# A hybrid decoder step: the tokens of the second part in two halves, the recurrence over all heads for each half

## The chip, the cores and the metric

One core of one Trainium2 chip runs the whole step as one program. The metric is the device time of that program in microseconds; lower is better. The engines are named as in the profile: PE (TensorE products), PEld (its loads of weights), DVE (VectorE), ACT (ScalarE), POOL (GpSimd) and SP (SyncE, which here issues nearly every DMA).

## The reference

One layer, 1024 prompt tokens and 8 samples of 4 tokens each (1056 columns), width 1024, in float32:

```
z = rmsnorm(x) @ w_in                       # conv inputs, r k v and LoRA inputs, two gates
ya = silu(layernorm(dwconv31(glu))) @ w_conv_out
xs = z_r + (shifted(z_r) - z_r) * mu        # token shift, then r, k, v, decay w, a, g
S_t = S_{t-1} diag(w_t) + (S_{t-1} a_t) b_t^T + v_t k_t^T ;  y_t = S_t r_t   # per head, 16 heads of 64
yb = ((groupnorm(y) + bonus) * g) @ w_rw_out
x = x + (sig(g1) * ya + sig(g2) * yb) @ w_mix_out
up = rmsnorm(x) @ w_up ; cu = dwconv3(up) ; x = x + (gelu(cu_1) * cu_2) @ w_down
out = rmsnorm(x), and the new conv, shift, wkv and ffn states
```

Only the recurrence over `S_t` and the two causal convolutions tie a token to those before it. Everything after the recurrence works on tokens by themselves, but for the three taps of the feed-forward's convolution, which need two earlier columns.

## The kernel before

Products in float32 precision are three products of rounded halves: each operand is split into a high and a low part, and `mm3` (a helper; all its products stand on line 54) sums high x high, high x low and low x high. Weights come by tiles: `wjob` (L47 to L49) loads 512 KB into `wraw`, ACT writes the high part `whi`, POOL the low part `wlo`. A tile of the weights is multiplied with all 1056 tokens in three blocks of 352 columns.

The program has three stages. First the input norm and `mixer_a`: convolution inputs, its taps on DVE, the LoRA parts and r, k, v of the first two tiles of channels. Then `mixer_b`, the recurrence. It is cut into 16 steps `n`: two pairs of heads (`J = n // 4`) and a quarter of the prompt (`q = n % 4`, 256 tokens in four chunks of 64). A step goes through `prep` (decays P on L904, the operands E and BK), `stage` (products of the keys into LQ; then the inverses of the 32 x 32 diagonal blocks, by 31 pairs of DVE operations on `tm` and `X`, L1027 and L1029, with round trips through DRAM before and after), `combine`, `chain` (the recurrence over the four chunks, whose output `Yev` is written on L1152) and `group_norm`. E, BK and LQ lie in the pool `stage` with three buffers. The samples' recurrence and the layer norm of the convolution run beside it. Last comes the tail: the conv branch's output (`conv_out`), `merge`, `mix`, and the feed-forward `ffn` by groups of three tiles (`ffn_up`, `ffn_down`), with the final norm in `ffn_last`. Intermediate results of all tokens go through DRAM (`d_ma`, `d_x2`).

The order of `mixer_b` is set by a planner, `drive` (L701). It holds a list of streams, each a generator that yields the time for which it has to wait, and a clock that counts products alone. The first stream that is due gets its turn; where none is, a step of a filler product is put in between. Fillers are the 18 remaining tiles of r, k, v and the 16 tiles of the gates, which are held back by `due` until a chain far enough ahead is done. Step `n` is prepared only after `chain(n - 3)`. The planner only gives the order of emission; the framework's scheduler then places the instructions of each engine by that priority and by readiness, and the engines run them in order.

The waiting times of a step by the planner:

```
W_NIN, W_BV, W_GN, W_STAGE = 6000, 8000, 12000, 0     # ns, in prep and group_norm
TINV = 29750                                          # from the end of stage to combine
LAT = (950, 1050, 1200)                               # in chain, for each of four chunks, 800 ahead
if n > 2:
    k.append(("chain", n - 3))                        # s_prep
```

Of the kernel before, what the change touches and what calls it, by code (L numbers as in the profile page):

```python
# [18 lines left out]
NB = 3  # L19
# [11 lines left out]

class Net:
# [7 lines left out]
    # ---------------------------------------------------------------- helpers  # L40
# [34 lines left out]
    def project_g(self, w, x, nk, evac, m=128):  # L75
        """products of one tile of the weights with all tokens; yields after every step of the contraction"""
# [12 lines left out]
    def project(self, *a, **k):  # L89
        self.run(self.project_g(*a, **k))  # L90

    def split_tok(self, b, ps, prompt, sample):
        """block b of the tokens: prompt(columns, psum) and sample(psum as batch x 4)"""
        t0 = b * BW
        n = min(TP - t0, BW)
        prompt(t0, n, ps[:, :n])
        if n < BW:
            sample(ps[:, n:BW].rearrange("p (b t) -> p b t", t=4))

    # ------------------------------------------------------------------ build  # L100
    def build(self):
        with ExitStack() as es:
# [4 lines left out]
            self.hL = self.hp.tile([128, 8, T], F32R, name="hL")  # L107
            self.wp = self.pool(es, "weights", 2)
            with ExitStack() as e1:
                self.rp = self.pool(e1, "wraw", 1)  # L110
                with ExitStack() as e:
                    self.pm = self.pool(e1, "pm", 4, space=PSUM)
                    self.pw = self.pool(e1, "pw", 2, space=PSUM)
                    xs, w0 = self.load_in(e)
                    self.norm_in(e, xs)
                with ExitStack() as e:
                    self.t4 = self.pool(e, "t4", 8)
                    self.mixer_a(w0)
                self.mixer_b()
            self.rp = self.pool(es, "wraw2", 2)  # L120
            self.tail()

    def consts(self, e):
# [18 lines left out]
        # vectors: rows of 128 in DRAM, turned on the tensor engine  # L142
# [29 lines left out]
    def turn(self, gi):  # L172
        """vectors of a group, by partitions"""
# [23 lines left out]
    # --------------------------------------------------- input norm, transposed  # L197
# [53 lines left out]
    # ------------------------------------------------ first part of the mixer  # L251
    def mixer_a(self, w0):
# [9 lines left out]
        self.d_ma, self.d_ga, self.d_gb, self.d_y = dram("d_ma"), dram("d_ga"), dram("d_gb"), two("d_y")  # L262
# [29 lines left out]
    def weave(self, main, *aux):  # L292
        """steps of the products, and between them those of the others, each at its rate from when it is ready"""
# [18 lines left out]
    def conv_start(self, e):  # L312
        """histories of the samples, by rows"""
# [10 lines left out]
    def conv_proj(self, cv, i, w=None):  # L324
        """gated inputs of the convolution, tile i of the channels"""
# [24 lines left out]
    def conv_taps(self, cv, i):  # L350
# [11 lines left out]
        # samples: all taps, then their sum  # L362
# [7 lines left out]
        # new buffers  # L370
# [14 lines left out]
    NLN, LNW = 8, 132  # L385

    def ln_block(self, b):
        """layer norm of the convolution's channels and twice their silu, for one block of the tokens"""
        nc = self.nc
        W = self.LNW  # L390
        s = slice(b * W, (b + 1) * W)
# [3 lines left out]
        def fold(t):  # L395
            """sum of the four channel tiles, in Q"""
# [21 lines left out]
    def conv_in(self):  # L418
        """the conv branch's inputs, in the room of the recurrence"""
        nc = self.nc  # L420
        self.e_sg.close()
        self.cvp = self.pool(self.e_sg, "conv", side="right")
        self.cs = [self.cvp.tile([128, 4, T], F32R, name=f"cs{x}") for x in "HL"]
        for b in range(NB):
            s = slice(b * BW, (b + 1) * BW)
            c = self.cvp.tile([128, 4, BW], F32, tag="cs", name="cs", bufs=2)
            nc.sync.dma_start(out=c, in_=self.d_cs[:, :, s])
# [4 lines left out]
    def conv_out(self, i):  # L432
# [6 lines left out]
        if i < ND - 1:  # L439
            self.cw = job(i + 1)  # L440
# [1238 lines left out]
```

## Time and profile before

| | |
|---|---|
| median of 3 runs | 2597.11 us (2591.31 to 2606.79) |
| profiled execution, span | 2603.0 us; the page gives no other time for it |
| PE busy | 2437.3 us, 94% |
| DVE, ACT, POOL busy | 1535.1, 913.1 and 914.3 us |
| moved by DMA | 230.62 MB, 89 GB/s on average |

The profile is of one execution. Busy time is the time in which an engine has an instruction in flight. The granted clock is given as a share of the full 2.4 GHz; the half level is 1.2 GHz. Products are pipelined, so a busy PE isn't PE at its peak. Some records of products are missing (2568 of the large products with `hH` stand where the code issues more), so that durations are read from runs of them on the chain of waits. A row of a group of instructions has the line, the engine, the operation, output and inputs by the program's names, count, busy time and mean.

### The profile page before, as it was taken

What the parts mean: (1) busy time and instruction counts of PE and PEld (TensorE: products, weight loads), DVE (VectorE), ACT (ScalarE), POOL (GpSimd) and SP (SyncE); (2) the same over time, 40 slices, a digit from 0 to 9 for tenths busy, and PEclk for the clock granted to TensorE, in tenths of its full rate; (3) what the DMA queues carried; (4) which work ended last, traced back from release to release, by engine and by line L of the source; (5) the groups of instructions that cost most, each with busy time, mean ns of one, the idle gap of its engine ahead of it and who ended that gap; (6) DMA issues with size and microseconds to landing.
All of it is one profiled execution on the core that took longest, in us unless ns stands there. A gap on an engine that the chain in (4) does not pass through costs nothing.

```text
span 2603.0 us, 41626 instructions
## 1 busy us (share of the span) xinstructions
PE 2437.3 (94%) x16094; PEld 2182.3 (84%) x16094; DVE 1535.1 (59%) x3588; ACT 913.1 (35%) x1732; POOL 914.3 (35%) x879
## 2 busy tenths in 40 slices
PE   6899989989899889999898999999999999999998
PEld 5788977767787767777666899999999999999998
DVE  5999765677675866655655434455444435444445
ACT  4234342344254344344343412333222212222225
POOL 3432261334333524433232224333323323232343
PEclk9999977688786888787688999999999999999999
DMA  4124442233232333433333564441111111111111
GB/s 120 53 68 167 159 113 76 76 92 103 77 95 84 91 83 93 108 83 78 81 98 79 189 228 144 116 158 51 36 54 45 44 48 43 47 51 38 54 45 74
DMA packets 307638, 230.62 MB, mean 89 GB/s; under 512 B 90492, under 2 KB 287123, under 8 KB 306921
## 3 DMA queue, kind: packets, MB, share of 16 engines
q1 hardware_dynamic: 307185, 227.80, 29.8%
q8 instruction: 127, 2.08, 0.3%
q14 instruction: 70, 0.57, 0.1%
q0 software_dynamic: 256, 0.17, 0.0%
HBM read 157.45 MB, written 70.45 MB: 88 GB/s over the span
## 4 chain that ended last, share of the span: by engine, by line
PE 65%; DVE 14%; DMA 3%; issue 1%; SPq 1%; ACT 1%; POOL 1%; ACTq 0%; POOLq 0%; DVEq 0%
PE mm L54 51%; PE w L54 6%; DVE tm L1027 4%; DVE X L1029 4%; PE c L54 3%; PE y L54 3%; DMA L<-dL 2%; PE w L61 2%; DMA dX<-X 1%; DVE UV L1142 0%; DVE E L922 0%; DVE E L981 0%; SPq L1031 0%; DVE UV L1131 0%; DVE t L961 0%
## 5 line engine op out<-in xcount | busy, mean ns | idle before, releaser
L54 PE MATMUL mm<-hH,whi 128*128 128x352 f32 (+1 forms) x2568 | 900.6, 351 | 23.0 <-DVE bcol L496 13.1
L54 PE MATMUL mm<-hH,wlo 128*128 128x352 f32 (+1 forms) x2568 | 882.0, 343 | 0.0
L54 PE MATMUL mm<-hL,whi 128*128 128x352 f32 (+1 forms) x2568 | 880.6, 343 | 0.3 <-DVE hL L248 0.3
L54 PEld LDWEIGHTS mm<-hH,whi 128*128 128x128 f32 (+1 forms) x2568 | 508.3, 198 | 53.0 <-issue 20.1
L54 PEld LDWEIGHTS mm<-hL,whi 128*128 128x128 f32 (+1 forms) x2568 | 510.3, 199 | 13.4 <-issue 1.1
L54 PEld LDWEIGHTS mm<-hH,wlo 128*128 128x128 f32 (+1 forms) x2568 | 509.6, 198 | 13.3 <-issue 0.9
L49 POOL TENSOR_TENSOR wlo<-wraw,whi 128x1024 fp32r<-128x1024 f32 (+2 forms) x123 | 295.6, 2403 | 413.6 <-ACT whi L48 377.9
L48 ACT ACTIVATE whi<-wraw 128x1024 fp32r<-128x1024 f32 (+2 forms) x123 | 126.0, 1024 | 338.6 <-PE mm L54 231.7
L1541 DVE SCALAR_TENSOR_TENSOR c<-u,par,c 128x1024 f32<-128x1024 f32 x96 | 167.0, 1739 | 55.9 <-ACT c L1537 55.9
L1027 DVE TENSOR_TENSOR tm<-L,X 128x60 f32<-128x60 f32 (+24 forms) x496 | 168.0, 339 | 41.1 <-DMA L<-dL 33.5
L359 DVE SCALAR_TENSOR_TENSOR sg<-cu,par,sg 128x1024 f32<-128x1024 f32 x120 | 185.4, 1557 | 2.7 <-ACT sg L357 1.7
L1511 DVE TENSOR_TENSOR u<-mm,rs 128x352 f32<-128x352 f32 x144 | 73.2, 509 | 186.2 <-PE mm L54 186.1
L1029 DVE TENSOR_TENSOR X<-X,tm 128x60 f32<-128x60 f32 (+24 forms) x496 | 178.6, 360 | 6.9
L1566 DVE TENSOR_TENSOR acc<-mm,acc 128x352 f32<-128x352 f32 x168 | 86.7, 522 | 135.0 <-PE mm L54 135.0
L54 PE MATMUL mm<-fH,whi 128*128 128x352 f32 x504 | 163.4, 324 | 0.0
L54 PE MATMUL mm<-fH,wlo 128*128 128x352 f32 x504 | 162.8, 323 | 0.0
L54 PE MATMUL mm<-fL,whi 128*128 128x352 f32 x504 | 162.7, 323 | 0.0
L1011 POOL TENSOR_SCALAR_AFFINE_SELECT LQ<-LQ 64x512 f32<-64x512 f32 x64 | 44.3, 693 | 180.3 <-ACT LQ L1007 180.1
L1102 ACT ACTIVATE SP<-UV,PC 64x64 f32<-64x64 f32 x192 | 64.5, 343 | 117.8 <-DVE UV L1142 102.5
L1522 POOL COPY lr<-u 128x2 f32<-128x2 f32 x48 | 8.9, 184 | 275.5 <-DVE u L1511 266.8
L54 PE MATMUL w<-E,BK 64*128 64x128 f32 x512 | 93.9, 339 | 2.4 <-DVE t L969 1.4
L54 PEld LDWEIGHTS mm<-fH,whi 128*128 128x128 f32 x504 | 94.8, 188 | 0.5
(378 smaller groups left out, 4002.0 us busy)
## 6 DMA issues: line engine op xcount, KB each, us to landing
wraw<-w_in SPq DMA_DIRECT2D x50, 512.0 KB
wraw<-w_up SPq DMA_DIRECT2D x48, 512.0 KB
wraw<-w_down SPq DMA_DIRECT2D x32, 384.0 KB
L<-dL SPq DMA_DIRECT2D x16, 512.0 KB
d_alr<-la SPq DMA_DIRECT2D x8, 528.0 KB
d_gout<-lg SPq DMA_DIRECT2D x8, 528.0 KB
d_cum<-lc SPq DMA_DIRECT2D x8, 528.0 KB
d_k<-k SPq DMA_DIRECT2D x8, 528.0 KB
```

What stands on the lines that cost most here:

```text
L48: nc.scalar.activation(out=hi[:, :nk, :m], in_=raw[:, :nk, :m], func=AF.Copy)
L49: (lo_eng or nc.gpsimd).tensor_tensor(out=lo[:, :nk, :m], in0=raw[:, :nk, :m], in1=hi[:, :nk, :m].bitcast(F32), op=ALU.subtract)
L54: self.nc.tensor.matmul(out, l, r, start=start, stop=stop)
L61: self.nc.tensor.transpose(out, x, ident)
L359: nc.vector.scalar_tensor_tensor(out=c[:, 0:TP], in0=u[:, t:t + TP], scalar=self.col("conv_w", t * 4 + i), in1=c[:, 0:TP], op0=ALU.mult, o ...
L1011: nc.gpsimd.affine_select(out=w, in_=w, pattern=[[0, 4], [1, 2], [1, 64]], compare_op=ALU.is_ge, fill=0.0, base=-1, channel_multiplier=-1)
L1027: nc.vector.tensor_tensor(out=tm[:, :a, :m], in0=L[:, s:s + 1, s + 1:32].to_broadcast([128, a, m]), in1=X[:, :a, s:s + 1].to_broadcast([12 ...
L1029: nc.vector.tensor_tensor(out=X[:, :a, s + 1:32], in0=X[:, :a, s + 1:32], in1=tm[:, :a, :m], op=ALU.add)
L1102: nc.scalar.activation(out=at(SP, u, x), in_=src(x)[:, u], func=AF.Copy, scale=PC[hs[x], 4 * u + c:4 * u + c + 1])
L1511: nc.vector.tensor_tensor(out=u[:, 2 + t0:2 + t0 + m], in0=p, in1=rs[:, t0:t0 + m], op=ALU.mult)
L1541: nc.vector.scalar_tensor_tensor(out=c[:, 0:TP], in0=u[:, t:t + TP], scalar=wt, in1=c[:, 0:TP], op0=ALU.mult, op1=ALU.add)
L1566: nc.vector.tensor_tensor(out=acc[i][:, s], in0=ps[:, :BW], in1=acc[i][:, s], op=ALU.add)
```

## The change

All columns from the merge on are split into two halves, `HALVES`: prompt tokens 0 to 511 (one block of 512), and 512 to 1023 with the 32 sample columns (two blocks of 272). The steps are numbered anew: 0 to 7 are the first two quarters of all heads, 8 to 15 the last two. The state of each pair of pairs is kept in `carry[J]`. The fillers, once r, k, v and gates are through, go on with the whole rest of the first half: conv branch and merge, mix, feed-forward and final norm. The tail does the same for the second half. `hist` keeps the two last columns of each tile of `up` for the second half's taps. The first half's gated operands lie in the room of the inputs (`hH`, `hL`), which is free once the gates are done. To make room, the pool `stage` gets two buffers in place of three, the small tiles `t2` 11 in place of 12, and a step is prepared after `chain(n - 2)`. `mixer_b` gets two buffers for raw weights in place of one. The feed-forward's groups have four tiles in place of three. Weights from `w_conv_out` to `w_down` are loaded and split once for each half. `d_ma` and `d_x2` go.

```diff
+HALVES = Half(0, (512,), False), Half(512, (272, 272), True)
+    def half_g(self, H, w, x, nk, evac):
+        wh, wl = w
+        for b, (o, n) in enumerate(H.blocks):
+            ps = self.pm.tile([128, 512], F32, tag="mm", name="mm")
+            for k in range(nk):
+                self.mm3(ps[:, :n], (wh[:, k], wl[:, k]), x(k, slice(o, o + n)), k == 0, k == nk - 1)
+                if k < nk - 1:
+                    yield 0
+            evac(b, slice(o, o + n), ps[:, :n])
+            yield 0
...
+    def JQ(n):
+        h, i = divmod(n, 8)
+        return i // 2, 2 * h + i % 2
...
-    T2N = 12
+    T2N = 11
...
-            self.sg = self.pool(self.e_sg, "stage", 3, side="right")
+            self.sg = self.pool(e, "stage", 2, side="right")
...
-            k = [("rkv", j, x) for j in (n // 4 * 2, n // 4 * 2 + 1) for x in range(3)]
-            if n > 2:
-                k.append(("chain", n - 3))
+            J, q = self.JQ(n)
+            k = [("rkv", j, x) for j in (2 * J, 2 * J + 1) for x in range(3)]
+            if n > 1:
+                k.append(("chain", n - 2))
...
     def fillers(self):
         gates = [(i, x) for x in range(2) for i in range(ND)]
-        due = lambda: len(gates) > 2 * ND - self.GATE0 or ("chain", 2 * ND - len(gates) - self.GATE0) in self.done
         tiles = [(j, x) for j in range(2, ND) for x in range(3)]
...
+        while tiles:
+            yield from self.rkv_tile(*tiles.pop(0))
+        while gates:
+            yield from self.gate(*gates.pop(0))
+        self.done.add("gates")
+        H = HALVES[0]
+        e = self.e_b
+        while "samples" not in self.done:
+            yield 1
+        self.e_a.close()
+        rs = self.pool(e, "half", side="right").tile([128, 512], F32, name="rsA")
+        wk = self.pool(e, "work", 6, side="right")
...
+            while not all(("ln", b) in self.done for b in range(4)):
                 yield 1
+            cs = [cs.tile([128, 4, 512], F32R, name=f"csA{x}") for x in "HL"]
+            self.conv_in(H, cs, w)
+            while not all(("yA", J) in self.done for J in range(ND // 2)):
+                yield 1
+            yield from self.merge(H, y, cs, m, w)
+        acc = self.pool(e, "accA", side="right")
+        acc = [acc.tile([128, 512], F32, name=f"accA{i}") for i in range(ND)]
+        u = y
+        yield from self.mix(H, m, u, acc, rs, w)
+        f = lambda k: tuple(t[:, k, 512:1024] for t in h)
+        yield from self.ffn(H, u, acc, rs, f, w)
+        yield from self.finish(H, acc, w)
...
-    SQ = (1, 1, 2, 1)
+    SQ = (0, 0, 1, 1)
...
-    G = 3
+    G = 4
...
+                else:
+                    nc.gpsimd.tensor_copy(out=self.hist[:, j], in_=z[:, 512:514])
```

## Rows read from the trace of the kernel before

**Rows 1.** Stages of the program: stretch, length, busy of each engine, clock, DMA.
```profile
core 0: us, PE busy (x) PEld busy (x) DVE busy (x) ACT busy (x) POOL busy (x), PEclk, DMA share, GB/s
326.00:1476.00 1150.00, 1033.80 (x7558) 833.57 (x7557) 744.66 (x2381) 470.18 (x1058) 420.60 (x442) 0.80 0.34 91
1476.00:2603.00 1127.00, 1113.38 (x6915) 1092.49 (x6913) 514.65 (x845) 320.45 (x465) 384.27 (x340) 0.99 0.25 79
```

**Rows 2.** Chain of waits in the tail: start us, us, products of 352, 384, 288 columns.
```profile
1909.34 11.67 PE mm L54 x72
...
2569.95 3.17 PE mm L54 x18
...
2587.60 2.39 PE mm L54 x18
```

**Rows 3.** Line 1152, a step's end: duration min/median/max, first and last start.
```profile
L1152 ACT ACTIVATE Yev<-y x16: 597/597/598, 465.9 to 1459.2; 128x512 f32<-128x512 f32 x16
```

**Rows 4.** Costliest groups of the page: count, busy us, mean ns, idle before.
```profile
L49 POOL TENSOR_TENSOR wlo<-wraw,whi 128x1024 fp32r<-128x1024 f32 (+2 forms) x123 | 295.6, 2403 | 413.6 <-ACT whi L48 377.9
L48 ACT ACTIVATE whi<-wraw 128x1024 fp32r<-128x1024 f32 (+2 forms) x123 | 126.0, 1024 | 338.6 <-PE mm L54 231.7
...
L1027 DVE TENSOR_TENSOR tm<-L,X 128x60 f32<-128x60 f32 (+24 forms) x496 | 168.0, 339 | 41.1 <-DMA L<-dL 33.5
...
L1029 DVE TENSOR_TENSOR X<-X,tm 128x60 f32<-128x60 f32 (+24 forms) x496 | 178.6, 360 | 6.9
```

**Rows 5.** Chain of waits near 371 us: a load of weights on it.
```profile
371.40 4.91 DMA wraw<-w_in
```

**Rows 6.** Waits of SP's queue, 326 to 1476 us: us, times, longest.
```profile
SPq L47 <- POOL wlo L49: 48.2, 10, 11.8
```

**Rows 7.** Line 49 (low parts of weights) alone, same stretch: POOL busy (count), clock, DMA.
```profile
326.00:1476.00 1150.00, 76.18 (x32) 0.80 0.34 91
```

**Rows 8.** Timeline near 392 us, DVE and POOL: start us, us.
```profile
392.22 0.23 DVE L1029 TENSOR_TENSOR X<-X,tm 128x70 f32<-128x70 f32 x1
...
392.49 2.45 POOL L49 TENSOR_TENSOR wlo<-wraw,whi 128x1024 fp32r<-128x1024 f32 x1 [6.11 <-ACT whi L48]
...
392.75 2.28 DVE L1029 TENSOR_TENSOR X<-X,tm 128x65 f32<-128x65 f32 x1
```

**Rows 9.** Line 1029: duration ns min/median/max, first and last start.
```profile
L1029 DVE TENSOR_TENSOR X<-X,tm x496: 119/214/2401, 376.8 to 1416.4; 128x60 f32<-128x60 f32 x16, 128x28 f32<-128x28 f32 x12, 128x66 f32<-128x66 f32 x11, 128x48 f32<-128x48 f32 x10
```

**Rows 10.** Chain of waits, shares of the span by line.
```profile
PE mm L54 51%; PE w L54 6%; DVE tm L1027 4%; DVE X L1029 4%; PE c L54 3%; PE y L54 3%; DMA L<-dL 2%; PE w L61 2%; DMA dX<-X 1%; DVE UV L1142 0%; DVE E L922 0%; DVE E L981 0%; SPq L1031 0%; DVE UV L1131 0%; DVE t L961 0%
```

**Rows 11.** Slices of 50 us, large products alone: PE busy (count), the others, clock.
```profile
476.00:526.00 50.00, 23.06 (x69) 15.01 (x67) 2.53 (x8) 1.66 (x3) 0.64 0.23 63
...
576.00:626.00 50.00, 28.22 (x123) 21.28 (x123) 4.99 (x17) 2.72 (x5) 0.90 0.37 95
...
776.00:826.00 50.00, 20.19 (x58) 12.49 (x57) 2.37 (x8) 1.08 (x2) 0.63 0.19 53
...
926.00:976.00 50.00, 27.68 (x131) 22.87 (x132) 0.99 (x4) 1.92 (x4) 0.84 0.37 92
...
1426.00:1476.00 50.00, 33.46 (x170) 27.10 (x170) 0.00 (x0) 3.13 (x7) 0.98 0.49 145
```

**Rows 12.** Timeline of ACT: ends of chains 8 and 11, P of steps 11 and 15.
```profile
1020.12 0.60 ACT L1152 ACTIVATE Yev<-y 128x512 f32<-128x512 f32 x1 [3.39 <-PE y L54]
...
1054.29 0.61 ACT L904 ACTIVATE P<-cum 128x512 f32<-128x512 f32 x1
...
1228.09 0.60 ACT L1152 ACTIVATE Yev<-y 128x512 f32<-128x512 f32 x1 [1.52 <-PE y L54]
...
1336.95 0.61 ACT L904 ACTIVATE P<-cum 128x512 f32<-128x512 f32 x1
```

**Rows 13.** The slice at 776 us with all instructions, columns as in rows 1.
```profile
776.00:826.00 50.00, 44.55 (x300) 32.99 (x299) 29.03 (x77) 17.39 (x42) 16.13 (x17) 0.63 0.19 53
```

More of the change, by code (lines that the diff above doesn't have):

```diff
@@ L29, with __init__ @@
 DEC = math.exp(-0.5)
+class Half:
+    def __init__(self, c0, widths, samples):
+        self.c0, self.W, self.samples = c0, sum(widths), samples
+        self.blocks = [(sum(widths[:b]), w) for b, w in enumerate(widths)]
+HALVES = Half(0, (512,), False), Half(512, (272, 272), True)
 class Net:
@@ L795, in s_samples @@
             yield from one(self.samples_state(j), 3)
+        self.done.add("samples")
     def s_ln(self):
-        for b in range(self.NLN):
+        for b in range(len(self.LNB)):
             yield from self.wait(("chain", b))
@@ new lines, in tail @@
+            w = lambda nm: wk.tile([128, 568], F32, tag="w", name=nm)
+            u = tuple(t[:, :, 512:T] for t in h)
+            with ExitStack() as em:
+                mp = self.pool(em, "mB", side="right")
+                m = [mp.tile([128, 8, H.W], F32R, name=f"mB{x}") for x in "HL"]
+                with ExitStack() as e2:
+                    yp = self.pool(e2, "yB")
+                    y = [yp.tile([128, 8, H.W], F32R, name=f"yB{x}") for x in "HL"]
+                    cs = [yp.tile([128, 4, H.W], F32R, name=f"csB{x}") for x in "HL"]
+                    self.conv_in(H, cs, w)
+                    for J in range(ND // 2):
+                        j = slice(2 * J, 2 * J + 2)
+                        nc.sync.dma_start(out=y[1][:, j].bitcast(F32), in_=self.d_y[J][:, :, H.c0:T])
+                        self.split(y, (slice(None), j), y[1][:, j].bitcast(F32))
+                    self.run(self.merge(H, y, cs, m, w))
+                ap = self.pool(e, "accB")
+                acc = [ap.tile([128, H.W], F32, name=f"accB{i}") for i in range(ND)]
+                self.run(self.mix(H, m, u, acc, rs, w))
@@ L1400, in mix, with norm @@
+    def mix(self, H, m, u, acc, rs, w):
         nc, a = self.nc, self.a
[L1401 to L1404 removed]
+        ssum = w("ssum")
+        x = lambda k, s: (m[0][:, k, s], m[1][:, k, s])
+        xk = self.load_xk(H, 0, w)
+        def norm(s):
             ps = self.pw_tile()
[L1406 to L1409 removed]
@@ L1411, in mix @@
[L1411 to L1422 removed]
+            n = s.stop - s.start
```

531 lines of the change are left out of this document (252 added, 279 removed).

## The prediction

> **What bounds the kernel now.** I read the busy time by stage first, then the spacing of one step of the recurrence, then the clock against the products in slices, and last the rows of single instructions. The stages [rows 1]: a head to 326 us, a middle of 1150 us in which the recurrence runs, and a tail of 1127 us. In the tail PE is busy 1113 of 1127 us at a clock of 0.99: it is bound by PE and nothing else. In the middle PE is busy 1034 of 1150 us, but the granted clock is 0.80 on average. A clock of 0.80 is 40% of the time at 1.2 GHz and 60% at 2.4. So the middle holds 1150 x 0.80 = 920 us at the full clock, of which 116 us are idle, and 804 us of PE work. The clock takes 230 us and idle time 116: these 346 us, 22 for each of the 16 steps (n), are all that a better order can win, since the change takes no products away.
>
> The 804 us are 34 filler tiles (18 of k, r, v, 16 gates) and the recurrence's own products. A tile is 72 matmuls, 11.67 us [rows 2], so 34 are 397 us; the recurrence with its samples is 407, or 25 us for each n. Steps end 66 us apart: (1459.2 - 465.9) / 15 [rows 3]. Of these 66 us, 25 are filler.
>
> **The change part by part.**
>
> *Products.* A half of the tokens is one block of 512 columns, or two of 272. The trace has 352, 384 and 288 columns: 11.67 / 72 = 162 ns, 3.17 / 18 = 176 and 2.39 / 18 = 133 [rows 2], which is 0.45 ns for a column. This gives 234 ns at 512 and 126 at 272, both an estimate, since no row has these widths. Output, mix and feed-forward are 8 x 12 + 8 x 8 + 48 x 8 + 24 x 8 = 736 steps of the contraction with three products for each block. Before: 736 x 9 x 0.162 = 1073 us. After: 736 x 3 x 0.234 = 516 us for the first half and 736 x 6 x 0.126 = 556 for the second. The sum stays; 516 us leave the tail and go into the middle. The tail becomes 1127 - 1073 + 556 = 610 us.
>
> *Weights twice.* Each of these 96 tiles of weights is loaded and split once more: ACT 1.02 us, POOL 2.4 us [rows 4] and 512 KB (half of it for 8). In the tail a tile of w_up is now used up in 48 x 0.126 = 6.0 us where it was 11.7. POOL and ACT keep pace, and two raw buffers hide the load, which took 4.91 us where it stood on the chain [rows 5]. I cost it at nothing; without that cover a tile would take 4.9 + 1.0 + 2.4 = 8.3 us, 2.3 more, 200 us over the 88 large tiles. In the middle the tiles' loads stand in SP's queue ahead of the loads of the next step and of its lane inverse. SP waited for a raw buffer 10 times there, 48 us in all, for 32 tiles [rows 6, 7]; three times as many more make 145 us at that rate, with a second raw buffer in the middle to lower it. On the path I take none; both ends go into the range.
>
> *VectorE beside GpSimd.* The second half of the middle gets the splits (88 x 2.4 + 8 x 1.2 = 221 us) and some 50 us of products and copies on POOL. An X step of the inverse took 0.23 us, and 2.28 when a wlo of 2.45 us ran on POOL [rows 8]. All 992 X and tm instructions took 347 us [rows 4]; at 0.21, the median of X [rows 9], they would be 208. So 139 us were lost beside 421 us of POOL [rows 1], a third; 271 us more of POOL make 89 us more. This is between nothing and 89 us on the path. X and tm hold 8% of the chain of waits, 208 us [rows 10], and PE is the one that waits in only a tenth of the middle, so I take 24 us, the low quarter. The Trainium skill ("SBUF — State Buffer", "Who interferes with whom") says that a VectorE instruction with two SBUF inputs and a GpSimd instruction that reads SBUF lock each other out for the whole instruction. The row agrees; by the rule at its worst all 271 us are lost and the sum is 247 higher (a rival below).
>
> *The order.* The first half starts only when all gates, the samples' state and the group norms of n = 0 to 7 are emitted, and the planner serves the recurrence before it. By its own waiting times a step takes 6 + 8 us of prep, 29.75 of inverse, 2.2 of combine and some 13 of chain, with products between about 85 us, so a pair lasts about 90 and the fillers get half of it. The gates are then through near n = 10, and part of the first half's feed-forward is left when the recurrence ends. I take 200 us of the 516 as left over; the ends are 0 and 516. What is left runs as the tail does now, at the full clock.
>
> *Clock and idle.* In slices of 50 us the clock follows the count of large products: 69 give 0.64, 123 give 0.90, 131 give 0.84, 170 give 0.98 [rows 11]. After the change the middle has 397 + 516 - 200 = 713 us of filler beside 16 steps, 45 us each. At some 84 us a step that is 27 us in 50, as much as 165 products of 162 ns. Between the rows of 131 and 170 I take 0.92, below the straight line, because a slow clock also lowers the count. Idle time I leave at 116 us: the same steps wait for the same engines.
>
> *Small.* Row buffers of the convolution's state in place of whole-token tiles add 48 POOL copies near 0.2 us; the dropped DRAM round trips of the gated conv branch and of x were behind dense products: nothing. Two new seams, from gates to the first half (group norm, loads, splits) and from its final norm to the second, cost PE 15 and 20 us, by the idle time of the present seam (1127 - 1113 = 14 us in the whole tail); ends 0 and 60.
>
> *The buffers.* E, LQ and BK go from three to two, the small tiles from 12 to 11, and prep(n) waits for chain(n-2), not n-3. Now P of prep(11) comes at 1054.3, 34 us after chain(8) ended at 1020.1, and chain(11) ends at 1228.1 [rows 12]: a loop of 208 us for three steps in flight. The last step, with little beside it, needs 1337.0 to 1459.2, 122 us. Two in flight so give between (122 + 26) / 2 = 74 and 104 us a step (26 us being about the usual gap). My 84 lies inside, nearer the low end since two steps disturb each other less than three. As long as filler is at hand a longer step costs PE nothing.
>
> **The sum.** Middle: (804 + 516 + 116 - 200) / 0.92 + 200 + 24 = 1567 us. Head 326, tail 610, seams 35: 2538 us against a span of 2603.0. The page gives the span alone as the profiled execution's time; it is 5.9 us above the median of 2597.1 and within the three runs, so I take 6 off: 2532.
>
> **The rivals.**
>
> *A. Two buffers set the pace (slower).* If a step takes the upper 104 us, the recurrence ends at 466 + 15 x 104 = 2026 us, and seams and tail make 2671, or 2665. For it: prep follows chain(n-3) so closely. Against: the 122 us, and PE's share in the loop's time. It decides from a step of (2603 - 645 - 466) / 15 = 99 us.
>
> *B. The two don't run beside each other, or the loss belongs to the step and not to its density.* Then the middle stays 1150 and 516 follow at the full clock: 326 + 1150 + 516 + 645 = 2637, or 2631. For it: the planner's order, and slices like that of 776 us, where the clock is 0.63 [rows 11]. Against: 0.98 at 170 products.
>
> *C. The clock stays full.* Middle 804 + 516 + 116 + 24 = 1460: 2431, or 2425; with idle time down to 3 us a step, 2357. The Trainium skill ("TensorE: Matmul & The Clock Gate", "Part 1: The HAM clock gate") says that the default is throttled and activity releases it. Against: in the slice at 776 us PE is busy 44.55 of 50 us and the clock is 0.63 [rows 13], so a busy PE alone does not bring it.
>
> *D. VectorE is locked out for all of POOL's new time*: 2532 + 247 = 2779. Against: two thirds of POOL's time now cost X nothing.
>
> **Chances.** Forecast (2460 to 2590 by its bounds of clock 0.88 to 0.98 and leftover) 0.43, A 0.19, B 0.13, C 0.20, D 0.05. About 0.5% (13 us) is what a measurement can tell from no change. Faster: 0.40 of the forecast and all of C, 0.60. Within 0.5%: 0.03 of the forecast and 0.05 of B, 0.08. Slower: A, D and 0.08 of B, 0.32. The range leaves out the low part of C and the top of A and D: 2380 to 2680; the forecast's own is 2460 to 2590.
>
> **What would show it.** Right: the clock of the middle over 0.9; large products of 512 columns at 234 ns beside the recurrence; Yev 80 to 90 us apart; a tail near 610 us at full clock. Wrong: Yev over 99 us apart with PE idle (A); a middle at 0.80 with the first half's feed-forward as a dense stretch after the last Yev (B); X at 0.6 us and PE waiting for it (D). A tail slower than 6.0 us for a tile of w_up would mean that the weights' loads are not hidden, which would falsify the step on weights.

## The result, and the profile after

The changed kernel takes 2695.07 us (median of 4 runs, 2675.66 to 2698.62) against 2599.66 for the kernel before in the same measurement: a ratio of 1.034 (95% interval 1.029 to 1.040). It is slower. The prediction said 2532 (2380 to 2680) and gave slower a chance of 0.32. The profiled execution has a span of 2673.9 us; it was the fastest of the four runs.

The stages after, columns as in [rows 1]: the recurrence to its last step; the first half's products that were left, up to its final norm; the seam to the second half, with the last 80 of these products; the rest.

```profile
326.00:1616.00 1290.00, 1125.78 (x8245) 907.89 (x8246) 831.25 (x2425) 519.32 (x1123) 508.73 (x487) 0.85 0.35 97
1616.00:2012.00 396.00, 374.04 (x1587) 296.43 (x1588) 214.86 (x221) 133.39 (x168) 202.88 (x184) 1.00 0.31 94
2012.00:2120.00 108.00, 94.52 (x613) 87.88 (x612) 45.90 (x84) 38.96 (x58) 50.94 (x37) 0.91 0.47 143
2120.00:2673.00 553.00, 535.67 (x4116) 518.95 (x4114) 317.30 (x590) 213.91 (x366) 272.85 (x280) 0.99 0.29 85
```

The middle grew from 1150 to 1290 us at a clock of 0.85 (before 0.80), and 396 us at full clock follow it. By the prediction's ledger the middle loses 1290 - 1126 = 164 us to idle time and 0.15 x 1290 = 193 to the clock, 357 in all or 22.3 for each step; before it was 346, or 21.6 [rows 1]. So what the change was to win back is all still there. (The ledger counts idle time that falls at half clock as a loss of clock too, so further down elapsed times are the surer measure.) The reader sees why in the products of 512 columns, of which the first half has 736 x 3 = 2208. In the time from the last gate (its store is issued at about 1265 us) to the last step, the groups of PE by form, with count, busy us and mean ns:

```profile
L65 PE MATMUL mm<-hH,whi 128*128 128x512 f32 x152 | 73.3, 482 | 0.7 <-ACT whi L59 0.7
L65 PE MATMUL mm<-hL,whi 128*128 128x512 f32 x151 | 68.5, 453 | 1.4 <-DVE hL L1405 1.4
L65 PE MATMUL mm<-hH,wlo 128*128 128x512 f32 x151 | 68.1, 451 | 6.2 <-POOL wlo L60 6.2
...
L65 PE MATMUL mm<-csAH,whi 128*128 128x512 f32 x32 | 14.0, 439 | 0.0
```

That is 454 with `hH` or `hL` and three times 32 of the conv branch: 550 of 2208, a quarter. The same rows of the dense stretch from 1616 to 2012 us:

```profile
L65 PE MATMUL mm<-hH,wlo 128*128 128x512 f32 x527 | 210.3, 399 | 19.6 <-POOL wlo L1623 11.1 <-POOL wlo L60 8.5
L65 PE MATMUL mm<-hL,whi 128*128 128x512 f32 x527 | 208.7, 396 | 0.0
L65 PE MATMUL mm<-hH,whi 128*128 128x512 f32 x527 | 207.6, 394 | 0.0
```

1581 of them, with 20 us of waiting for low parts; the kernel before waits 1.9 us for them in its whole tail. Steps end (1615.9 - 449.2) / 15 = 77.8 us apart [rows 3], and X and tm did not slow down [rows 4]:

```profile
L1171 ACT ACTIVATE Yev<-y x16: 577/598/603, 449.2 to 1615.9; 128x512 f32<-128x512 f32 x16
...
L1047 DVE TENSOR_TENSOR tm<-L,X 128x60 f32<-128x60 f32 (+24 forms) x496 | 151.5, 305 | 86.5 <-DMA L<-dL 74.7
L1049 DVE TENSOR_TENSOR X<-X,tm 128x60 f32<-128x60 f32 (+24 forms) x496 | 155.9, 314 | 12.1
```

### The profile page after: what moved, and what is told of

The parts are those of the page before. It is cut to its first block, busy times and chain, and to the rows that moved or that the text cites. A ratio compares the mean times of both kernels' runs of the same rounds, so it can differ in the third digit from the quotient of the medians.

```text
span 2673.9 us, 42600 instructions
## 1 busy us (share of the span) xinstructions
PE 2405.5 (90%) x16094; PEld 2053.3 (77%) x16094; DVE 1682.1 (63%) x3678; ACT 1028.2 (38%) x1923; POOL 1139.5 (43%) x1087
## 5 line engine op out<-in xcount | busy, mean ns | idle before, releaser
L65 PE MATMUL mm<-hH,whi 128*128 128x352 f32 (+2 forms) x2696 | 967.4, 359 | 14.3 <-DVE bcol L492 9.6
L65 PE MATMUL mm<-hH,wlo 128*128 128x352 f32 (+2 forms) x2696 | 940.7, 349 | 27.9 <-POOL wlo L60 16.8
L65 PE MATMUL mm<-hL,whi 128*128 128x352 f32 (+2 forms) x2696 | 938.5, 348 | 1.6 <-DVE hL L1405 1.4
L60 POOL TENSOR_TENSOR wlo<-wraw,whi 128x1024 fp32r<-128x1024 f32 x195 | 461.3, 2367 | 533.6 <-ACT whi L59 454.4
L65 PEld LDWEIGHTS mm<-hH,wlo 128*128 128x128 f32 x2696 | 527.5, 196 | 78.9 <-POOL wlo L60 22.8
L65 PEld LDWEIGHTS mm<-hH,whi 128*128 128x128 f32 x2696 | 526.8, 195 | 74.7 <-issue 22.9
L65 PEld LDWEIGHTS mm<-hL,whi 128*128 128x128 f32 x2696 | 527.9, 196 | 42.5 <-issue 3.0
L1592 DVE SCALAR_TENSOR_TENSOR c<-u,par,c 128x512 f32<-128x512 f32 (+1 forms) x288 | 301.5, 1086 | 109.1 <-ACT c L1585 107.5
L59 ACT ACTIVATE whi<-wraw 128x1024 fp32r<-128x1024 f32 x195 | 197.8, 1015 | 252.2 <-PE mm L65 212.8
L1623 POOL TENSOR_TENSOR wlo<-wraw,whi 128x1024 fp32r<-128x1024 f32 x44 | 105.2, 2395 | 43.7 <-ACT whi L1622 40.9
L65 PE MATMUL mm<-fBH,whi 128*128 128x272 f32 x320 | 93.2, 291 | 0.0
```

The lines of the kernel that those rows point to most:

```text
L59: nc.scalar.activation(out=hi[:, :nk, :m], in_=raw[:, :nk, :m], func=AF.Copy)
L60: (lo_eng or nc.gpsimd).tensor_tensor(out=lo[:, :nk, :m], in0=raw[:, :nk, :m], in1=hi[:, :nk, :m].bitcast(F32), op=ALU.subtract)
L65: self.nc.tensor.matmul(out, l, r, start=start, stop=stop)
L1592: add = lambda o, i: nc.vector.scalar_tensor_tensor(out=o, in0=i, scalar=wt, in1=o, op0=ALU.mult, op1=ALU.add)
L1623: (lo_eng or nc.gpsimd).tensor_tensor(out=lo, in0=raw, in1=hi.bitcast(F32), op=ALU.subtract)
```

## The experiments

Five things could carry the 95 us: the third buffer that was given up (depth), how much of the first half stands beside the steps (density, the forecast's own mechanism, against a loss that belongs to each step whatever stands beside it: per step), the new order of the heads, the seams and the weights that are split twice, and GpSimd's splits beside VectorE (lock). All times are medians; a ratio is to the kernel before in the same measurement.

### Depth and density on the kernel before: e1 and e4

```diff
-self.sg = self.pool(self.e_sg, "stage", 3, side="right")
+self.sg = self.pool(self.e_sg, "stage", 2, side="right")
-if n > 2: k.append(("chain", n - 3))
+if n > 1: k.append(("chain", n - 2))
```

> The kernel before with two buffers in place of three for E, LQ and BK, and prep(n) waiting for chain(n-2); nothing else. If the depth of the buffers is what the change pays for (theory depth), steps lengthen from 66 us towards the 78 of the kernel after and the time rises by most of the 95 us between the two kernels: 2650 to 2700. If the loss belongs to how much filler stands beside a step (theory density), the 97 us of products that were left after the last step move between the steps, which longer waits no longer leave open: 2580 to 2620, steps of 70 to 74 us. If each step loses 22 us whatever stands beside it (theory per step), 2600.

2685.95 us, 1.035 (1.032 to 1.038). With its order untouched, two buffers cost the kernel before as much as the whole change did. Its middle, and the wait that took the place of the others (PE's waits there: us, times, longest):

```profile
326.00:1560.00 1234.00, 976.22 (x7591) 811.42 (x7590) 733.88 (x2373) 472.68 (x1061) 420.44 (x441) 0.78 0.32 85
```
```profile
PE w L54 <- DVE D L1065: 121.1, 14, 26.3
```

`D` is the tile `D11`, the first operation of `combine`, which waits for the inverse's round trip through DRAM. With two steps in flight PE stands there 14 times; before, this line took 3.4 us. Idle time goes from 116 to 258 us, and steps are 74.3 us apart.

But this isn't the price of depth by itself, because the fillers ran out. The first twelve steps and the last four, first with all instructions, then the last four with the large products' tile `mm` alone, and PE's longest wait there:

```profile
326.00:1286.00 960.00, 832.50 (x6272) 702.33 (x6271) 581.44 (x1862) 380.79 (x848) 345.62 (x363) 0.84 0.34 92
1286.00:1560.00 274.00, 143.72 (x1321) 109.10 (x1320) 152.44 (x512) 91.89 (x214) 74.82 (x79) 0.60 0.24 63
```
```profile
1286.00:1560.00 274.00, 3.27 (x12) 2.24 (x10) 0.00 (x0) 0.45 (x1) 0.60 0.24 63
```
```profile
PE w L54 <- DVE D L1065: 83.0, 4, 26.3
```

The last four steps have 12 large products between them, where those of the kernel before have 437. Their clock is 0.60, they hold 130 of the 258 us of idle time, and 4 of the 14 waits for `D`, 83 of the 121 us, are theirs. In the changed kernel, whose last steps have products of the first half beside them, the same line has only 8.7 us. That more filler is the reason was not tested by itself.

The control, waiting times of the planner times 1.3 in the kernel before:

```diff
-                x[1] = self.clock + wait
+                x[1] = self.clock + 1.3 * wait
```

> Control: the kernel before with the planner's waiting times multiplied by 1.3. By the written order the gates then end with the last step, where 97 us of products were left over. Theory density: the left-over 97 us go between the steps, the clock of the middle rises from 0.80 to about 0.84 and the time falls by 25 to 50 us: 2550 to 2575. Theory per step: no change, 2590 to 2610.

2589.02 us, 0.996 (0.992 to 0.999). Some 11 us less: short of the 25 to 50 that density said, and just under the range of per step. By the ledger its middle still loses 23 us a step.

### Density in the changed kernel: e2, e3, e7

e2 was to keep the first half apart from the recurrence by its place in the order of emission:

```diff
-        while "samples" not in self.done:
+        while "samples" not in self.done or ("gn", self.NH - 1) not in self.done:
```

> The kernel after, with the first half's output and feed-forward held back until the last group norm of the first-half and second-half steps is done, so that nothing of the halves stands beside the recurrence. Theory per step: the loss beside 16 steps stays at about 355 us, so the time stays at 2680 to 2710. Theory density: the 112 us of output and mix that stood beside steps 10 to 15 are gone from there, the clock of the middle falls from 0.85 to about 0.80 and idle time rises, 30 to 60 us lost: 2725 to 2755. Theory depth: as density, more of it idle time than clock.

2716.62 us, 1.047 (1.042 to 1.051), between the ranges of the theories. It held back only a part: the first product of the conv branch starts at 1307.1 us, beside step 11 as in the changed kernel (1287.1), and 384 of the 550 products of 512 columns still stand before the last step. The framework's scheduler had moved them up to where they were ready. e5 keeps the halves apart properly.

e3 multiplies all waiting times of the planner by 1.6, e7 those of the recurrence's own five streams alone:

```diff
-        live = [[g, 0.0] for g in streams]
+        live = [[g, 0.0, 1.6 if i < 5 else 1] for i, g in enumerate(streams)]
...
-                x[1] = self.clock + wait
+                x[1] = self.clock + x[2] * wait
```

> The kernel after, with every waiting time of the planner multiplied by 1.6, which puts more products between two steps of the recurrence: by the written order 955 of the middle's 1145 us (at the planner's own prices) stand before the end of the last step, where it was 788. Theory density: the dense stretch after the recurrence falls from 396 to about 200 us, the clock of the middle rises from 0.85 to 0.92 or more and idle time falls: 2560 to 2620. Theory per step: the loss stays at 355 us, 2680 to 2710, only the dense stretch is shorter and the steps are longer. A third outcome: between the end of the gates and the first half's output there are four steps with no products beside them (some 100 us of waiting by the planner), which would take back what density gives: 2650 to 2700 with a stretch of low clock there.

> The kernel after, its two buffers kept, with the waiting times of the recurrence's own streams multiplied by 1.6 and those of the samples, the conv norm and the y loads as they were; by the written order 1010 of 1145 us stand before the end of the last step (788 in the kernel after), without the starved stretch that all waits times 1.6 had. Theory density: 2590 to 2625, the dense stretch after the last step near 150 us. Theory per step: as with all waits times 1.6, 2640 to 2660.

e3: 2646.63 us, 1.020 (1.016 to 1.023), in none of its three ranges; the starved stretch of its third outcome is there, two steps from 1069 to 1208 us without one large product, at a clock of 0.55. e7: 2625.58 us, 1.012 (1.006 to 1.017): 69 us under the changed kernel, from the order alone, at the upper edge of what density said. The middle and the stretch left after the last step in e7:

```profile
326.00:1826.00 1500.00, 1275.03 (x9277) 1048.53 (x9278) 952.83 (x2560) 615.60 (x1240) 636.21 (x609) 0.89 0.36 99
1826.00:1974.00 148.00, 140.34 (x599) 111.08 (x600) 79.19 (x92) 55.10 (x72) 80.53 (x68) 1.00 0.35 105
```

The rest went from 396 to 148 us and the clock to 0.89, but idle time went from 164 to 225 us. By the ledger the loss is then 390 us, 24 a step; by elapsed time the middle and the rest together, which hold nearly the same products, went from 1290 + 396 = 1686 to 1648 us. So density moved the clock, and idle time took a part of it back.

### The halves by themselves: e5, e9, e16

e5 has three buffers, and runs the first half as a stretch of its own after the recurrence's pools are closed, which makes the room.

```diff
-self.sg = self.pool(e, "stage", 2, side="right")
+self.sg = self.pool(e_r, "stage", 3, side="right")
...
             self.drive([...], self.fillers())
+            self.e_a.close()
+            e_r.close()
+            self.rp = self.pool(self.e_b, "wrawA", 2, side="right")
+            self.run(self.half_a())        # what fillers() did after the gates
```

> The kernel after with three stage buffers again (prep(n) waits for chain(n-3)), and the first half's output, feed-forward and final norm run as a stretch of their own once the recurrence is through and its buffers are released, so that both fit. It has the halves, their widths and their twice loaded weights, but neither the two buffers nor anything of the halves beside the recurrence. Theory depth (the 86 us that two buffers cost the kernel before are the regression): the halves by themselves cost only their seam and some products more, 2600 to 2630. If the halves themselves are the price (weights loaded twice, seams, POOL), 2660 to 2720.

2744.79 us, 1.060 (1.052 to 1.067), above both ranges: the halves by themselves are a price. A part of it is a middle that runs out of filler, as in e1: its last three steps have 26 large products and a clock of 0.55.

```profile
1360.00:1502.00 142.00, 7.23 (x26) 5.38 (x25) 0.00 (x0) 0.93 (x2) 0.55 0.18 49
```

e9 is e5 with the old order of the heads:

```diff
-        h, i = divmod(n, 8)
-        return i // 2, 2 * h + i % 2
+        return divmod(n, 4)                 # JQ; NQ likewise 4 * J + q
```

> The kernel with three buffers and the halves apart, with the recurrence in the order of the kernel before again (pair by pair, four steps each) in place of all heads for one half, then the other. What is left of the change is the two halves of output, feed-forward and final norm, one after the other. Theory heads: in the order by halves all k, r, v tiles (18 tiles, 210 us) are due within the first 8 steps and hold them up, 83 us a step there against 69 before; with the old order this goes and the time falls by 40 to 70 us, to 2680 to 2700. Theory seams and weights (idle time of the dense stretches, 66 us more than before): the rest stays, 2660 to 2690 here, so 60 to 90 above the kernel before. If the heads' order is free: 2730 to 2760.

2708.67 us, 1.040 (1.033 to 1.047): some 36 us less by the medians (51 by the ratios), the intervals just apart. Steps are (1470.9 - 478.5) / 15 = 66.2 us apart, as before [rows 3], where e5 has (1501.6 - 447.3) / 15 = 70.3: all k, r, v are due within eight steps in the new order, and the last steps of e5 are left without. What remains of e9 is the tail in two halves: its PE waits from 1471 us on, where the kernel before is idle 14 us in the whole tail [rows 1]:

```profile
PE mm L65 <- POOL wlo L60: 22.1, 23, 1.8
PE mm L65 <- POOL wlo L1623: 13.2, 11, 2.2
PE mm L65 <- ACT csBH L1404: 10.0, 1, 10.0
PE w L72 <- POOL Yev L1239: 7.0, 1, 7.0
```

e16 takes the first two away: in the two halves of e9 the low parts are made on VectorE.

```diff
+        self.lo_eng = self.nc.vector        # from half_a on
...
-        (lo_eng or nc.gpsimd).tensor_tensor(
+        (lo_eng or self.lo_eng or nc.gpsimd).tensor_tensor(
```

> The kernel with three buffers, the old order of the heads and the halves apart (2709 us), with the low parts on VectorE in the two halves alone; the middle is untouched. If the weights' splits hold up the dense halves (PE waited 34 us for wlo there, and 66 us were idle that the kernel before hasn't): 2650 to 2680. If the cost is in the seams: 2690 to 2710.

2645.80 us, 1.014 (1.006 to 1.022), 63 us less. From 1489 us to the end PE is idle 36 us where e9 was idle 79 from 1471:

```profile
1489.00:2651.00 1162.00, 1125.98 (x6917) 1008.18 (x6916) 670.58 (x1141) 447.13 (x666) 200.96 (x363) 0.98 0.35 105
```
```profile
1471.00:2686.00 1215.00, 1136.04 (x6919) 1006.36 (x6918) 639.98 (x954) 440.61 (x666) 612.49 (x551) 0.98 0.34 100
```

So of some 107 us that the halves cost by themselves, 40 to 60 are the splits of their weights on GpSimd, which are made once for each half: 63 by the medians, 53 by the two stretches, 43 by their idle time. The rest, some 45 to 65, is left for the seams and what else the halves bring.

### Three buffers with the first half beside: e8 and e6

The changed kernel with its third buffer back, the first half's residual sum and gated conv branch in DRAM for room, and the waits of the recurrence's streams times 1.6 (e8) or 2 (e6):

```diff
+                    x = w("acc")[:, 0:512]
+                    nc.sync.dma_start(out=x, in_=acc[i])      # acc: DRAM tiles
...
+                    nc.sync.dma_start(out=acc[i], in_=x)
```

> As the kernel with three buffers beside the recurrence, with the recurrence's waits times 1.6 instead of 2: by the written order 807 of 1145 us before the end of the last step. Theory density: slower than with times 2 by 20 to 50 us. Theory per step: the same within 10 us.

> The change with three stage buffers and the first half beside the recurrence: room is made by keeping the first half's residual sum and its gated conv branch in DRAM (some 90 loads and 90 stores of 256 KB more, all of them beside products), one raw weight buffer until the half begins, and the waiting times of the recurrence's own streams (not of the samples) doubled, so that by the written order 894 of 1145 us stand before the end of the last step. Theory density (the loss falls as filler is added): clock of the middle over 0.92, 2480 to 2540. Theory per step with depth (16 steps lose 22 us each whatever stands beside them, and two buffers cost 86 us more): 2590 to 2630. If the DRAM detours cost on the path: up to 2680.

e8: 2603.11 us, 1.004 (1.000 to 1.008); e6: 2619.94, 1.011 (1.005 to 1.017), their intervals overlapping. e6 is in the range of per step with depth; density had e6 at 2480 to 2540 and e8 slower than it by 20 to 50 us. One of the three products with 512 columns (`hH` by `whi`), up to the last step, in e8, e6 and e7:

```profile
L74 PE MATMUL mm<-hH,whi 128*128 128x512 f32 x211 | 97.0, 461 | 0.7 <-ACT whi L68 0.7
```
```profile
L74 PE MATMUL mm<-hH,whi 128*128 128x512 f32 x348 | 155.4, 447 | 8.1 <-ACT whi L68 8.1
```
```profile
L65 PE MATMUL mm<-hH,whi 128*128 128x512 f32 x496 | 219.7, 443 | 6.6 <-DVE tm L1047 6.6
```

With the others of their kind that is 632 products before the last step in e8, 1042 in e6 and 1582 in e7, where the changed kernel has 550. So e8 has hardly more of the first half beside its steps than the changed kernel and is 92 us faster: the third buffer and the longer waits together go with that, and not the number of products. With 410 more of them e6 gains nothing. This number by itself, which is what density counts, does not set the time. Depth is not isolated either: e7 to e8 is 22 us with overlapping intervals, but e8 also has 950 products fewer beside the steps and the traffic to DRAM.

### GpSimd's splits: e10 to e14, e18

One edit in several kernels: the low part of each weight tile of the middle and the first half is made on VectorE (as in e16, from `mixer_b` to the tail).

> The kernel after, its order untouched, with the low parts of the middle's and the first half's weight tiles on VectorE. If GpSimd's splits are what the change pays for beside the recurrence, the time falls by as much as with the longer waits (113 us): 2570 to 2600. If they cost only where filler is dense beside the steps, less, since only 24 of the half's tiles stand beside steps here: 2620 to 2660.

> Control: the kernel before, its order untouched, with the low parts of the middle's 34 tiles on VectorE. As with waits times 1.3, 20 to 45 us less: 2555 to 2580. The gap between this and the changed kernel with the same edit is what the change costs without GpSimd's splits.

> The kernel after with the recurrence's waits times 1.6, and the low part of every weight tile of the middle made on VectorE in place of GpSimd. Theory lock: each wlo of 2.4 us on GpSimd holds X and tm up; with it gone X and tm fall from 0.3 to 0.21 us, the inverses end some 5 us earlier each and PE no longer waits for wlo in the dense stretch: 2560 to 2610. If VectorE is what the steps wait for (some 100 splits of about 1.2 us added to it): 2625 to 2660.

> The kernel before with waits times 1.3 and the low parts of the middle's 34 weight tiles on VectorE. Theory lock: 139 us of X and tm go against some 40 us of splits, of which a tenth to a third was on the path: 2560 to 2585. Theory VectorE: 2590 to 2610.

> Three buffers, the first half beside the recurrence, waits times 1.6, and the low parts of the middle's and the first half's weight tiles on VectorE. Theory lock: 2540 to 2590, the first version under the kernel before. Theory VectorE: 2600 to 2640.

> Three buffers, first half beside the recurrence, the recurrence's waits times 2, low parts on VectorE. With waits times 1.6 it took 2521 us with some 440 us of the first half left after the last step. Theory density: more of it beside the steps, 2470 to 2505. If the steps' own waits set the pace by now: 2515 to 2540.

| kernel | splits on GpSimd | on VectorE | ratio on VectorE |
|---|---|---|---|
| before | 2599.66 | 2561.47 (e14) | 0.983 (0.977 to 0.989) |
| before, waits 1.3 | 2589.02 (e4) | 2553.88 (e11) | 0.984 (0.978 to 0.991) |
| changed | 2695.07 | 2676.35 (e13) | 1.028 (1.019 to 1.036) |
| changed, waits 1.6 | 2625.58 (e7) | 2512.66 (e10) | 0.967 (0.962 to 0.972) |
| three buffers, waits 1.6 | 2603.11 (e8) | 2520.68 (e12) | 0.969 (0.964 to 0.973) |
| three buffers, waits 2 | 2619.94 (e6) | 2536.80 (e18) | 0.977 (0.970 to 0.984) |

In the changed kernel's own order no effect of the splits is shown (the intervals of e13 and of the changed kernel overlap). With the recurrence's waits times 1.6 they cost 113 us with two buffers, and 82 with three, where only 632 and 630 products of the first half stand beside the steps (e8, e12). So what they cost isn't set by this number either. Against the ranges: e13 is above both of its own, e14 inside, and e10, e11 and e12 are below theirs. e10 has nearly the middle that the prediction described; below it are the same stretches of e13:

```profile
326.00:1723.00 1397.00, 1245.23 (x9278) 1023.24 (x9279) 947.07 (x2665) 613.24 (x1237) 423.57 (x502) 0.93 0.38 106
1723.00:1860.00 137.00, 137.00 (x595) 110.62 (x594) 84.15 (x115) 55.39 (x72) 28.96 (x44) 1.00 0.37 113
```
```profile
326.00:1627.00 1301.00, 1140.41 (x8251) 909.42 (x8252) 818.13 (x2486) 522.04 (x1124) 378.50 (x425) 0.86 0.35 96
1627.00:2012.00 385.00, 382.18 (x1642) 308.27 (x1642) 229.65 (x294) 143.59 (x180) 69.40 (x121) 1.00 0.34 102
```

Clock 0.93, idle 152 us, so a loss of 152 + 98 = 250 us or 15.6 a step: in the changed kernel order alone gave 24 (e7) and the splits alone 21 (e13: 161 us idle and 0.14 x 1301). By elapsed time the middle and the rest take 1686 us in the changed kernel and in e13, 1648 in e7 and 1534 in e10: the two edits together give more than both by themselves. e10 beats both kernels and the best form of the kernel before (e11, intervals apart). A third buffer adds nothing to it: e12, with 630 products beside the steps where e10 has 1583, is 8 us slower, the intervals overlapping. More of them add nothing to e12: e18 has 1041, was expected at 2470 to 2505 by density and came out at 2537.

### Lock or queue: e15 and e17

X and tm together go from 332 us in e7 to 280 in e10, 52 us of a gain of 113, so the lock on these two is not all. GpSimd's queue is the rival. In e7 it stands for 251 us at low parts whose high part isn't there (us, times, longest), with the recurrence's masks and operands behind them:

```profile
POOL wlo L60 <- ACT whi L59: 251.2, 43, 20.2
```

e15 adds to e10 eight subtractions on GpSimd for each tile that depend on nothing:

```diff
+            for _ in range(8):
+                nc.gpsimd.tensor_tensor(out=self.junk, in0=self.ident, in1=self.ident, op=ALU.subtract)
```

> The fast version (two buffers, waits times 1.6, low parts on VectorE) with GpSimd's busy time put back: for each weight tile eight subtractions of 128x128 from SBUF, 2.5 us in all, that wait for nothing and that nothing waits for. Theory lock: VectorE is locked out as before and the time goes back up by 80 us or more, 2590 to 2630. Theory queue (GpSimd stands at a wlo that waits for its high part, 251 us in 43 waits, with the recurrence's work behind it): such work without a wait costs little, 2510 to 2550.

2899.13 us, 1.113 (1.105 to 1.120), and nothing is learned on the rivals: the scheduler put all of them into the first 700 us, as the page's row of GpSimd in 40 slices (72.5 us each) shows, and the head waited for GpSimd.

```profile
POOL 7889888987303234231423314242121354544444
```

e17 ties five of them to the weight tile before:

```diff
+            for k in range(5):
+                nc.gpsimd.tensor_tensor(out=self.junk, in0=self.last_hi[:, k % 4].bitcast(F32), in1=self.ident, op=ALU.subtract)
```

> The fast version (two buffers, waits times 1.6, low parts on VectorE, 2513 us) with five subtractions of 128x128 on GpSimd for each weight tile of the middle and the first half, 2.6 us in all by the 0.53 us that one took, that read the weight tile before (long split) and that nothing waits for. Theory lock: GpSimd's busy time beside the steps costs VectorE as the low parts did, 2590 to 2630. Theory queue: no wait for a fresh high part, so little is lost, 2515 to 2550.

2588.80 us, 0.995 (0.991 to 0.999), just under the range of lock and far above that of queue: 76 of the 113 us are back, although nothing waits for these results. The groups of e17:

```profile
L63 POOL TENSOR_TENSOR junk<-whi,ident 128x128 f32<-128x128 f32 x525 | 333.5, 635 | 277.8 <-ACT whi L60 237.2
...
L1056 DVE TENSOR_TENSOR tm<-L,X 128x60 f32<-128x60 f32 (+24 forms) x496 | 152.7, 308 | 113.0 <-DMA L<-dL 103.7
L1058 DVE TENSOR_TENSOR X<-X,tm 128x60 f32<-128x60 f32 (+24 forms) x496 | 156.2, 315 | 9.7
```

X and tm are up 29 us against e10, so these two are slowed by work on GpSimd as such, whatever it is for. But the queue stood at these too, 237 us for high parts, and they took 414 us with those of the second helper, more than the splits they replace. What is shown is that GpSimd's time beside the steps costs, in this order; how it divides between lock and queue stays open.

## Why the prediction was wrong

It put the end of the first half at 326 + 1567 = 1893 us. The final norm of its last tile starts at 2032:

```profile
L1669 ACT ACTIVATE accA<-accA,par x8: 721/724/726, 2012.4 to 2031.9; 128x512 f32<-128x512 f32 x8
```

What follows took 642 us, against 645 for seams and tail. So the whole of the 136 us by which the profiled span missed its 2538 lies before it; by the medians the miss is 163.

**The order: the term that was mis-sized, and the step that failed first.** "I take 200 us of the 516 as left over." 374 us of PE work were left in a stretch of 396, and some 19 more behind it. The gates were through near n = 10, as said. But the prediction then asked five or six steps to take 316 us of filler, 53 to 63 each, when its own rate was 45 a step and its own step of 84 us at a clock of 0.92 holds 77 - 25 = 52; at 45 some 270 would have been left. The trace has 550 products of 512 columns in 351 us there, 128 us at 0.233: about 25 a step. With 374 left in place of 200 the prediction's own formula gives a filler of (397 + 516 - 374) / 16 = 34 us a step. In the measured step of 77.8 us that is 133 products of 162 ns in 50 us, where the clock was 0.85 (the rows of 123 and 131 have 0.90 and 0.84 [rows 11]), and (804 + 516 + 116 - 374) / 0.85 + 374 + 24 = 1647: 80 of the 139 us up to 2032. e7 changes the order alone, leaves 148 us and brings 69 us.

That is a part of the miss and not the whole: e7, with less left over than was forecast, is at 2626 us still 94 above the forecast. With the splits off GpSimd as well e10 is 19 below it. So in e7's order the term on VectorE beside GpSimd, further down, is the other part: 113 us where 24 were taken. Nor does the rest by itself decide: e12 leaves 526 of each kind of product after its last step, the changed kernel 553, and e12 takes 2521 us.

**Idle time: wrong.** "Idle time I leave at 116 us." It was 164 beside the steps and 22 in the dense stretch. How much of this is the second buffer stays open. e1 has the price of two buffers in the kernel before, 86 us, but half of its idle time lies in four steps without filler, so that it doesn't refute "as long as filler is at hand a longer step costs PE nothing". e8, with a third buffer and longer waits, is 92 us under the changed kernel at nearly the same number of products beside the steps. No run has the third buffer alone in the changed kernel's order.

**Weights twice: wrong.** "I cost it at nothing." PE waited 20 us for low parts in the changed kernel's dense stretch and 7 after it, and e16 against e9 gives 40 to 60 us where both halves stand apart; without cover it was priced at 200. The sign that was named didn't come: six products in 0.75 us make 6.0 us for a tile of w_up, and the waits fall between tiles. The load was hidden; GpSimd's low parts were not.

**The new order of heads: not priced.** 36 us by e5 and e9, as far as their intervals allow, in kernels without the first half beside the steps.

**VectorE beside GpSimd: not seen in this order, and far too small for the one that was forecast.** +24 us were taken; X and tm lost 40 us less than before [rows 4], and e13 takes 19 us off, which its interval doesn't tell from nothing. With less left over than the prediction assumed, the same splits cost 113 us (e7, e10), above its bound of 89 and under D's 247. Only 52 of those are in X and tm, on which the bound was built. The Trainium skill ("SBUF — State Buffer", "Who interferes with whom") says that a VectorE instruction with two SBUF inputs contends with a GpSimd instruction that reads SBUF. e17's 29 us on X and tm agree with it, and no run here shows it to be the whole.

**Products: right; step and clock: near.** Consecutive products of the changed kernel (start us, busy us), first in the dense stretch, then in the second half:

```profile
1719.72 0.39 PE L65 MATMUL mm<-hH,whi 128*128 128x512 f32 x1
...
1721.58 0.40 PE L65 MATMUL mm<-hH,wlo 128*128 128x512 f32 x1
```
```profile
2399.71 0.29 PE L65 MATMUL mm<-fBH,wlo 128*128 128x272 f32 x1
...
2400.46 0.29 PE L65 MATMUL mm<-fBH,wlo 128*128 128x272 f32 x1
```

Eight products in 1.86 us are 233 ns and six in 0.75 are 125, against estimates of 234 and 126. Steps of 77.8 us lie in the 74 to 104, below the 84 that was taken. With about 140 us left over the clock is 0.93 in e10 and 0.89 in e7, against 0.92 for 200 left over.

**Rivals.** By number A's 2665 was nearest, then B's 2631. A's own sign, steps over 99 us, didn't come, so the number is no support for it. Of B's signs the feed-forward came as a dense stretch after the last step; the clock was 0.85 and not 0.80. The loss per step didn't move either (22.3 against 21.6), but it doesn't belong to the step: e10 has 15.6.

In sum, by medians and not additive: the halves apart cost some 107 us (e9), the order of heads some 36 (e5), and laying a quarter of the first half beside the steps, with two buffers, gave back some 50 (the changed kernel against e5). From there longer waits give 69 (e7), longer waits and a third buffer 92 (e8), and the splits off GpSimd after that 113 (e10) or 82 (e12).

## What to carry to other kernels

Before work is moved beside a latency-bound stage, count how much of it the order really puts before the stage's last step, and check by (work per step) x (steps left once the work may start) that it fits. Look for steps that are left without any: in e1, e3 and e5 they ran at a clock of 0.55 to 0.60. But the count alone doesn't give the time (e8 against e6 and the changed kernel). Room that is made by giving up a buffer can have a price of its own, to be measured alone first, in the order that is meant. And what the moved work brings along on side engines can hold up dense products (e9, e16) and can be most of the gain beside a stage that waits: test it in the target order, since the same edit was worth 19 us, not clear of nothing, in one order and 113 in another.

## What the runs showed of the hardware that was not expected

X has the same median in the changed kernel, e7 and e10 (215, 215 and 214 ns) while its longest is 2.43, 3.62 and 1.35 us: single instructions are held up and the usual one isn't slowed. The longest in the changed kernel lies beside a low part on GpSimd; but in e14, where the middle's low parts are on VectorE, one of 4.48 us lies beside other operations of GpSimd (on BK, lnC, lnQ and alr), so the splits are not the only work beside which this is seen. Rows of X by line (ns minimum/median/maximum), of the changed kernel and of e10, and the longest of e14 (start us, us):

```profile
L1049 DVE TENSOR_TENSOR X<-X,tm x496: 134/215/2426, 375.1 to 1568.4; 128x60 f32<-128x60 f32 x16, 128x28 f32<-128x28 f32 x12, 128x66 f32<-128x66 f32 x11, 128x48 f32<-128x48 f32 x10
```
```profile
L1051 DVE TENSOR_TENSOR X<-X,tm x496: 157/214/1353, 380.3 to 1671.1; 128x60 f32<-128x60 f32 x16, 128x28 f32<-128x28 f32 x12, 128x66 f32<-128x66 f32 x11, 128x48 f32<-128x48 f32 x10
```
```profile
743.39 4.48 DVE L1031 TENSOR_TENSOR X<-X,tm 128x49 f32<-128x49 f32 x1
```

The low part of a tile of 128x1024 took 2.4 us on GpSimd, and on VectorE in e10 1.32 us by one helper and 1.24 by the other.
